# Other places in SBUF for the operands of TensorE, in a two-block fp32 kernel on one core

## The chip, the cores and the metric

The kernel runs on one NeuronCore of a Trainium2 chip. The metric is the device time of one execution in microseconds. Engines are named as in the profile: PE (TensorE, matrix products), PEld (the loads of TensorE's stationary operand), DVE (VectorE), ACT (ScalarE), POOL (GpSimd), SP (the queue that issues most transfers).

## What is computed

Two transformer-like blocks run one after the other on 256 tokens of width 2048, all in fp32. What takes the time is the products with large weight matrices. Cut to these:

```python
z   = rmsnorm(x) @ w_in                          # 2048 -> 3392, then convolution and attention
x   = x + rmsnorm(concat(conv, attn) @ w_out)
ff  = silu(h @ w_gate) * (h @ w_up) @ w_down     # width 5632
x   = x + rmsnorm(ff)
p   = rmsnorm(x) @ w_in_2                        # then a pooling mixer and a linear recurrence
h   = x + concat(y_pool, y_lru) @ w_out_2
q   = z @ peer_wq                                # keys of 16384 experts, 8 heads, top 16 of each
out = rmsnorm(h + sum_k gate * gelu(u[expert] . z) * v[expert])
```

The last line is computed densely: all 16384 rows of `peer_u` are multiplied with the tokens, a matrix of gates that is zero outside the chosen experts is multiplied in, and the result is multiplied with all rows of `peer_v`.

## The kernel before

**Three products for one.** TensorE takes the operands of the large products as fp32r. Each fp32 operand is split into two such parts, `hi` (a copy by ACT, L140) and `lo` (the rest, a subtraction by DVE, L143). A product of two fp32 matrices is then three: hi by hi, hi by lo, lo by hi. Weights stream from HBM through `raw` (three buffers), and `hi` and `lo` have four buffers of 1024 columns each.

**Two forms of product.** A matmul instruction holds one operand still (the stationary one, 128 columns, loaded by LDWEIGHTS: 512 B in each partition) and streams the other (the moving one). In `unit_a` (L165 to L167) the weights are stationary and the 256 tokens move, so a product has 256 columns, 1024 B in a partition:

```python
T.matmul(o, hi[:, c], xh[:, kt, :], ...)   # L165: stationary hi, moving xh
T.matmul(o, hi[:, c], xl[:, kt, :], ...)   # L166
T.matmul(o, lo[:, c], xh[:, kt, :], ...)   # L167
```

In `unit_b` (L179 to L181) and in `products` (L1122) it is the other way round: 128 tokens are stationary and 512 columns of weights move, 2048 B in a partition. In the profile's names `acc<-znh,hi` the moving tile stands first and the stationary one second.

**Stages, in order.** `w_in` and `w_out` (both forms, until about 365 us), `w_gu` (`unit_a`, moving `lhi`/`llo`, until 857 us), `w_down` (`unit_b`, stationary `acth`/`actl`, until 1115 us), `w_in_2` (both forms, `z2h`/`z2l`), `w_out_2` (`unit_b`, `lhi`/`llo`), `peer_wq` (`unit_a`, `lhi`/`llo`), `peer_u` (`unit_a`, moving `znh`/`znl`, 1464 to 2219 us), `peer_v` (`products`, stationary `wsp`, from 2219 us to the end). Beside them run small products in plain fp32, and during `peer_u`, from 1625 to 1999 us, 256 one-hot products `gps` (L1043: moving `hb`, stationary `ha`, 256 columns) that build the gates. They stand in pairs among the products of `peer_u`.

**What sets the order.** The code records background work (`bg`, `heads`) between pieces of the weight stream, and a scheduler then orders each engine's instructions by its own simulation of time. Each engine runs its list in that order. A tile's buffers (`bufs`) limit how far ahead a writer may run.

**What sets the places.** Pools are laid one behind the other in each partition, and tiles within a pool likewise, so a tile's byte address is the sum of all that was opened before it. `lslot` cuts a view of 4096 columns out of a slightly larger tile, from column `off`; `lhs(16)` gives the view that begins 16 columns (64 B) further on. All slices that TensorE takes step by whole multiples of 512 B, except in one small unit of 320 columns, so each operand has one residue of its address modulo 512.

Of the kernel before, what the change touches and what calls it, by code (L numbers as in the profile page):

```python
# [10 lines left out]
F32 = mybir.dt.float32  # L11
F32R = mybir.dt.float32r
# [33 lines left out]
def build(tc, t, out, dbg=None, stop=None):  # L46

    nc = tc.nc
    dbg = dbg or {}
    top = ExitStack()  # L50
# [3 lines left out]
    cpool = top.enter_context(tc.tile_pool(name="cpool", bufs=1))  # L54
    stream = top.enter_context(tc.tile_pool(name="stream", bufs=1))

    gap = top.enter_context(tc.tile_pool(name="gap", bufs=1)).tile([128, 16], F32, name="gap")
    nc.vector.memset(gap, 0.0)
    lpool = top.enter_context(tc.tile_pool(name="lpool", bufs=1))
    small = top.enter_context(tc.tile_pool(name="small", bufs=4))  # L60

    x1d = dram.tile([128, 2, D], F32, name="x1d")
    hd = dram.tile([128, 2, D], F32, name="hd")
# [15 lines left out]
    def pc(name, j, n=1):  # L79
        o = COLS[name][0]  # L80
        return par[:, o + j:o + j + n]
# [88 lines left out]
    def unit_b(ps, w, xh, xl, nkt, n=512, k0=0):  # L170


        acc = [ps.tile([128, 512], F32, tag="acc", name="acc", bufs=4) for _ in range(2)]
        for kt, hi, lo in w.kts(nkt, n):
            for c in range(2):
                o = acc[c][:, :n]
                s = slice(c * 128, c * 128 + 128)
                k = k0 + kt
                T.matmul(o, xh[:, k, s], hi, start=(kt == 0), stop=False)  # L179
                T.matmul(o, xh[:, k, s], lo, start=False, stop=False)  # L180
                T.matmul(o, xl[:, k, s], hi, start=False, stop=(kt == nkt - 1))  # L181
        return acc
# [56 lines left out]
    def split(hi, lo, src):  # L239
        A.activation(hi, src, AF.Copy)  # L240
        V.tensor_tensor(lo, src, hi.bitcast(F32), op=ALU.subtract)
# [35 lines left out]

    def lslot(tag, name, shape, dt=F32R, off=0):

        x = lpool.tile([128, 4128 if tag == "lhi" else 4112], dt, tag=tag, name=name)[:, off:off + 4096]  # L280
        k = dict(zip("abc", shape))
        return x.rearrange("p (a b c) -> p a b c", **k) if len(shape) == 3 else x.rearrange("p (a b) -> p a b", **k)

    def lhs(off=0):
        return lslot("lhi", "lhi", (16, 256), off=off), lslot("llo", "llo", (16, 256), off=off)


    ps = tc.tile_pool(name="ps1", bufs=1, space=PSUM)
# [20 lines left out]
    kvn = p0.tile([128, 4, 256], F32, name="kvn")  # L309

    xgh, xgl = lhs()
    xTs = [slot(n, [128, 8, 256], name=f"xT{n}") for n in ("attn", "vt")]
    xsq = slot("sq", [128, 2, 4, 256], name="xsq")
# [138 lines left out]
    for c in range(2):  # L452
        A.activation(junk[:, :512], kvraw[:, c, :], AF.Square, accum_out=ssk[:, c:c + 1])
    rk = rstd_col(ssk[:, :2], 512, 2)
    mixh, mixl = lhs(16)


# [217 lines left out]
    nc.gpsimd.dma_start(grow, t["post_mix_norm"].partition_broadcast(128))  # L675
    r = proj((unit_b(ps, w, mixh, mixl, 8, k0=8) for _ in range(4)), p2, y, grow, half)
    hh, hl = lhs()
    r = rows(p2, add_residual(y, r, xt, y), y, hh, hl, "pre_ffn_norm")
    _, rb2 = to_row(lpool, r, "rb")
    nc.gpsimd.dma_start(x1d, y)  # L680
    dump("x1", y)
    if stop == "x1":
# [8 lines left out]

    p3x = ExitStack()
    p3 = p3x.enter_context(tc.tile_pool(name="p3", bufs=1))
    acth, actl = (p3.tile([128, 11296], F32R, name=n)[:, 16:11280].rearrange("p (k t) -> p k t", k=44)
                  for n in ("acth", "actl"))
    p3t = p3x.enter_context(tc.tile_pool(name="p3t", bufs=2))
    opt["pool"] = 0
# [1 line left out]
    for u in range(22):  # L699
# [7 lines left out]
        split(acth[:, 2 * u:2 * u + 2, :], actl[:, 2 * u:2 * u + 2, :], sg)  # L707
    grow = p3.tile([128, D], F32, name="grow3")
    y = lslot("lhi", "y3", (2, D), F32)
    x1 = lslot("llo", "x1r", (2, D), F32)  # L710
    nc.gpsimd.dma_start(x1, x1d)
    nc.gpsimd.dma_start(grow, t["post_ffn_norm"].partition_broadcast(128))
# [14 lines left out]
    t4 = t4x.enter_context(tc.tile_pool(name="t4", bufs=2))  # L727
# [95 lines left out]
    for u in range(2):  # L823
        acc = unit_b(ps, w, zh, zl, 16)
        for c in range(2):
            A.activation(ut[:, c, 512 * u:512 * u + 512], acc[c], AF.Copy, scale=r2[:, c:c + 1])
        for g in (2 * u, 2 * u + 1):
            dT = t4.tile([128, 2, 256], F32, tag="dT", name="dT")
            for i in range(2):
                ch = slice(256 * g + 128 * i, 256 * g + 128 * i + 128)  # L830
                dp = ps.tile([128, 512], F32, tag="tr", name="dp", bufs=4)
                T.matmul(dp[:, :256], ut[:, 0, ch], band[:, g, 0:256], start=True, stop=False)
                T.matmul(dp[:, 128:256], ut[:, 1, ch], band[:, g, 256:384], start=False, stop=True)
                V.tensor_copy(dT[:, i, :], dp[:, :256])
            for jt in range(2):
                yp = ps.tile([128, 512], F32, tag="tr", name="yp", bufs=4)
                for i in range(2):
                    T.matmul(yp[:, :256], pw[:, g, i, 128 * jt:128 * jt + 128], dT[:, i, :],  # L838
                             start=(i == 0), stop=(i == 1))
                k = 2 * g + jt  # L840
                yt = t4.tile([128, 256], F32, tag="yt", name="yt")
                V.tensor_scalar(yt, yp[:, :256], pc("pool_b_2", k), pc("pool_scale_2", k),
                                op0=ALU.add, op1=ALU.mult)
                split(yh[:, k, :], yl[:, k, :], yt)
# [157 lines left out]
    G = {}  # L1002
# [10 lines left out]
    NT = 8  # L1013
    hot = {}

    def iota8():
        return iota[:, None, :].to_broadcast([128, NT, 128])

    def over(x, g):
        return x[:, NT * g:NT * g + NT, None].to_broadcast([128, NT, 128])  # L1020

    def hot_a(g):
        a = G["hot"].tile([128, NT, 128], F32R, tag="ha", name="ha")
        hot[g] = [a]
        V.tensor_tensor(a, iota8(), over(slotT[:, 0, :], g), op=ALU.is_equal)

    def hot_e(g):
        e = G["hot"].tile([128, NT, 128], F32, tag="he", name="he")
        hot[g].append(e)
        V.tensor_tensor(e, iota8(), over(slotT[:, 1, :], g), op=ALU.is_equal)  # L1030

# [27 lines left out]
    for g in range(S // NT + 1):  # L1059
        first, last = g == 0, g == S // NT  # L1060
        for i, fn in enumerate((lambda g=g: hot_a(g), lambda g=g: hot_e(g),
                                lambda g=g: hot_b(g, 0), lambda g=g: hot_b(g, 1))):
            if not last:
                bg.append((1250, fn))
            if not first:
                bg.append((0, lambda g=g, i=i: meet(g - 1, i)))
                if i:
                    bg.append((700, lambda g=g, i=i: store(g - 1, i - 1)))
        if not first:
            bg.append((700, lambda g=g: store(g - 1, 3)))  # L1070
# [53 lines left out]
    for b in range(32):  # L1124
# [6 lines left out]
        for i in range(4):  # L1131
            x = (wh[:, i, :], wl[:, i, :], b == 0 and i == 0, b == 31 and i == 3)
# [144 lines left out]
```

## Time and profile before

| | us |
|---|---|
| median of 3 runs | 2948.01 (2947.69 to 2949.89) |
| the profiled execution | 2947.42 |
| its span (first to last instruction) | 2945.6 |
| PE busy in the span | 2905.0 |
| DVE busy | 1899.1 |
| ACT busy | 1326.9 |

The profiled execution is 0.6 us from the median. PE is recorded as busy when at least one matmul is in flight; matmuls overlap, one of 256 columns being in flight for some 280 ns while the next begins some 115 ns after it. So the busy time says that PE has work, not how fast it goes. How fast it goes is the spacing: the time from the start of one matmul to the start of the next. It is read from the timeline, or from the count of matmuls in a long stretch.

### The profile page before, as it was taken

The page shows a single profiled execution, that of the slowest core. Times are in us where ns is not written, and L with a number is a line of the kernel's source. Part 1 is how long each engine was busy: PE and PEld are TensorE (multiplying, and loading weights), DVE is VectorE, ACT ScalarE, POOL GpSimd, SP SyncE. Part 2 cuts the span into 40 slices and gives each one's busy share as a digit, 9 for nine tenths or more (in the row PEclk, how much of TensorE's full clock was granted, in tenths as well). Part 3 has the DMA queues.
Part 4 walks back from the last instruction along what each step waited for, and adds up shares of the span by engine and source line. Part 5 has one row for each costly group of instructions (what it writes and reads, how often), then busy time and mean ns, then how long its engine had stood idle before and what let it go on. Part 6 is the DMA issues. An engine that isn't in the chain of part 4 may idle for free.

```text
span 2945.6 us, 45194 instructions
## 1 busy us (share of the span) xinstructions
PE 2905.0 (99%) x18950; PEld 2640.4 (90%) x18950; DVE 1899.1 (64%) x2532; ACT 1326.9 (45%) x1638; POOL 28.4 (1%) x45
## 2 busy tenths in 40 slices
PE   8999999999999999999999999999999999999998
PEld 8887799999998888888999999999998888888886
DVE  7976655555554447857997988885445555555554
ACT  6226544444443435545444444444444444444443
POOL 0000000000000000000000000000000000000000
PEclk9999999999999999999999999999999999999999
DMA  6443555555565555465555666668657676667663
GB/s 238 165 150 129 214 196 186 187 188 188 187 215 186 187 194 215 152 220 207 174 206 215 231 220 252 220 254 296 214 209 264 230 240 239 235 232 239 231 217 138
DMA packets 120253, 615.72 MB, mean 209 GB/s; under 512 B 10320, under 2 KB 43216, under 8 KB 54768
## 3 DMA queue, kind: packets, MB, share of 16 engines
q1 hardware_dynamic: 116656, 574.16, 55.8%
q0 software_dynamic: 3392, 38.67, 3.3%
q8 instruction: 148, 2.42, 0.3%
q14 instruction: 57, 0.47, 0.1%
HBM read 570.85 MB, written 41.94 MB: 208 GB/s over the span
## 4 chain that ended last, share of the span: by engine, by line
PE 71%; issue 25%; DVE 3%; ACT 1%; DMA 0%; POOL 0%; SPq 0%; DVEq 0%; POOLq 0%; ACTq 0%
PE acc L167 16%; PE acc L165 16%; PE acc L166 16%; PE acc L180 6%; PE acc L181 6%; PE acc L179 6%; PE acc L189 2%; PE gps L1043 1%; DVE lo L143 1%; PE acc L198 0%; ACT junk L656 0%; PE yp L838 0%; PE scp L922 0%; PE sp L515 0%; DMA raw<-w_in 0%
## 5 line engine op out<-in xcount | busy, mean ns | idle before, releaser
L143 DVE TENSOR_TENSOR lo<-raw,hi 128x1024 fp32r<-128x1024 f32 (+1 forms) x968 | 1177.1, 1219 | 904.5 <-ACT hi L140 902.7
L140 ACT ACTIVATE hi<-raw 128x1024 fp32r<-128x1024 f32 (+1 forms) x968 | 1021.6, 1057 | 1403.2 <-PE acc L166 716.0
L167 PE MATMUL acc<-znh,lo 128*128 128x256 f32 x2048 | 570.7, 281 | 1.9 <-DVE lo L143 1.7
L166 PE MATMUL acc<-znl,hi 128*128 128x256 f32 x2048 | 572.0, 280 | 0.0
L165 PE MATMUL acc<-znh,hi 128*128 128x256 f32 x2048 | 572.0, 280 | 0.0
L1122 PE MATMUL o<-hi,wsp 128*128 128x512 f32 x2048 | 559.3, 395 | 0.0
L165 PE MATMUL acc<-lhi,hi 128*128 128x256 f32 x1856 | 522.5, 282 | 10.5 <-ACT hi L140 9.5
L167 PE MATMUL acc<-lhi,lo 128*128 128x256 f32 x1856 | 522.5, 283 | 1.2 <-DVE lo L143 1.2
L166 PE MATMUL acc<-llo,hi 128*128 128x256 f32 x1856 | 518.7, 280 | 0.9 <-DVE llo L253 0.9
L1122 PEld LDWEIGHTS o<-hi,wsp 128*128 128x128 f32 x2048 | 385.8, 188 | 89.9
L165 PEld LDWEIGHTS acc<-znh,hi 128*128 128x128 f32 x2048 | 391.1, 191 | 0.0
L167 PEld LDWEIGHTS acc<-znh,lo 128*128 128x128 f32 x2048 | 382.8, 188 | 3.4 <-DVE lo L143 3.3
L166 PEld LDWEIGHTS acc<-znl,hi 128*128 128x128 f32 x2048 | 384.5, 188 | 0.0
L165 PEld LDWEIGHTS acc<-lhi,hi 128*128 128x128 f32 x1856 | 349.3, 188 | 11.3 <-ACT hi L140 9.7
L166 PEld LDWEIGHTS acc<-llo,hi 128*128 128x128 f32 x1856 | 351.6, 189 | 1.4 <-DVE llo L253 1.4
L167 PEld LDWEIGHTS acc<-lhi,lo 128*128 128x128 f32 x1856 | 348.4, 188 | 2.1 <-DVE lo L143 2.1
L1122 PE MATMUL o<-lo,wsp 128*128 128x512 f32 x1024 | 321.2, 395 | 0.0
L1122 PEld LDWEIGHTS o<-lo,wsp 128*128 128x128 f32 x1024 | 192.9, 188 | 45.0
L181 PE MATMUL acc<-hi,actl 128*128 128x512 f32 x352 | 139.7, 397 | 0.0
L180 PE MATMUL acc<-lo,acth 128*128 128x512 f32 x352 | 139.4, 396 | 0.0
L180 PE MATMUL acc<-lo,lhi 128*128 128x512 f32 (+1 forms) x352 | 137.2, 390 | 0.0
L179 PE MATMUL acc<-hi,acth 128*128 128x512 f32 x352 | 136.9, 389 | 0.0
(339 smaller groups left out, 2725.7 us busy)
## 6 DMA issues: line engine op xcount, KB each, us to landing
raw<-peer_u SPq DMA_DIRECT2D x128, 1024.0 KB, 5.0
raw<-peer_v SPq DMA_DIRECT2D x128, 1024.0 KB, 5.6
raw<-w_gu SPq DMA_DIRECT2D x88, 1024.0 KB, 4.9
raw<-w_in SPq DMA_DIRECT2D x47, 1024.0 KB, 4.9
raw<-w_down SPq DMA_DIRECT2D x44, 1024.0 KB, 4.9
raw<-w_out SPq DMA_DIRECT2D x32, 1024.0 KB, 4.9
raw<-peer_wq SPq DMA_DIRECT2D x16, 1024.0 KB, 4.8
hD<-hg SPq DMA_DIRECT2D x32, 512.0 KB, 3.2
```

The source lines that it names most:

```text
L140: A.activation(hi[:, :m], raw[:, o:o + m], AF.Copy)
L143: e.tensor_tensor(lo[:, :m], raw[:, o:o + m], hi[:, :m].bitcast(F32), op=ALU.subtract)
L165: T.matmul(o, hi[:, c], xh[:, kt, :], start=(kt == 0 and m % 2 == 0), stop=False)
L166: T.matmul(o, hi[:, c], xl[:, kt, :], start=False, stop=False)
L167: T.matmul(o, lo[:, c], xh[:, kt, :], start=False, stop=(kt == nkt - 1 and m % 2 == 1))
L179: T.matmul(o, xh[:, k, s], hi, start=(kt == 0), stop=False)
L180: T.matmul(o, xh[:, k, s], lo, start=False, stop=False)
L181: T.matmul(o, xl[:, k, s], hi, start=False, stop=(kt == nkt - 1))
L189: T.matmul(acc[m // 2][:, m % 2, :], v[:, m * 128:m * 128 + 128], x(kt), start=(kt == 0 and m % 2 == 0), stop=(kt == nkt - 1 and m % 2 == 1))
L1043: T.matmul(o[:, j, :, :], a[:, 2 * p + j, :], b[:, 2 * p + j, :, :], start=True, stop=True)
L1122: T.matmul(acc[c][o // 512 + q], x[:, s], v[:, 512 * q:512 * q + 512], start=st, stop=sp)
```

## The change

Nothing that is computed changes. Places of tiles in SBUF change, and two tiles have one buffer in place of two. The parts: a pool of 64 B (`gap`) is gone; the pool `small` is opened ahead of `lpool`; the tiles `lhi`, `acth`, `actl` and `ha` are a little longer, with the view begun 16 columns in where they are stationary; `llo` has no offset any more; `yt` (pool mixer) and `he` (one-hot work) have one buffer.

```diff
-    gap = top.enter_context(tc.tile_pool(name="gap", bufs=1)).tile([128, 16], F32, name="gap")
-    nc.vector.memset(gap, 0.0)
+    small = top.enter_context(tc.tile_pool(name="small", bufs=4))
     lpool = top.enter_context(tc.tile_pool(name="lpool", bufs=1))
-    small = top.enter_context(tc.tile_pool(name="small", bufs=4))
...
-        x = lpool.tile([128, 4128 if tag == "lhi" else 4112], dt, tag=tag, name=name)[:, off:off + 4096]
+        x = lpool.tile([128, 4224 if tag == "lhi" else 4096], dt, tag=tag, name=name)[:, off:off + 4096]
...
-        return lslot("lhi", "lhi", (16, 256), off=off), lslot("llo", "llo", (16, 256), off=off)
+        return lslot("lhi", "lhi", (16, 256), off=off), lslot("llo", "llo", (16, 256))
...
-    acth, actl = (p3.tile([128, 11296], F32R, name=n)[:, 16:11280].rearrange("p (k t) -> p k t", k=44)
+    acth, actl = (p3.tile([128, 11392], F32R, name=n)[:, 16:11280].rearrange("p (k t) -> p k t", k=44)
...
-                yt = t4.tile([128, 256], F32, tag="yt", name="yt")
+                yt = t4.tile([128, 256], F32, tag="yt", name="yt", bufs=1)
...
-        a = G["hot"].tile([128, NT, 128], F32R, tag="ha", name="ha")
+        a = G["hot"].tile([128, 1152], F32R, tag="ha", name="ha")[:, 16:1040].rearrange("p (t k) -> p t k", t=NT)
...
-        e = G["hot"].tile([128, NT, 128], F32, tag="he", name="he")
+        e = G["hot"].tile([128, NT, 128], F32, tag="he", name="he", bufs=1)
```

The residues modulo 512 of the operands' byte addresses, as the two programs place them (M moving, S stationary):

| products | operand | before | after | the other operand |
|---|---|---|---|---|
| `unit_a`, 256 columns | M `lhi` | 0 | 384 | S `hi`, `lo`: 448 in both |
| | M `llo`, `znh`, `znl`, `z2h`, `z2l` | 128 | 384 | S `hi`, `lo`: 448 |
| `gps`, 256 columns | M `hb` | 128 | 384 | S `ha`: 128 before, 448 after |
| `products` of `peer_v`, 512 columns | S `wsp` | 64 | 448 | M `hi`, `lo`: 448 |
| `unit_b` of `w_down` | S `acth` | 192 | 448 | M 448 |
| | S `actl` | 320 | 448 | M 448 |
| `unit_b` of `w_out`, `w_out_2` | S `lhi` | 64 | 448 | M 448 |
| | S `llo` | 192 | 384 | M 448 |
| `unit_b` of `w_in` | S `lhi` / `llo` | 0 / 128 | 384 / 384 | M 448 |
| `unit_b` of `w_in_2` | S `z2h`, `z2l` | 128 | 384 | M 448 |
| plain fp32, 256 columns | M `qn`, `kvn`, `x32` | 128 | 384 | S `raw`: 448 |

The change moves instructions at two places only, where the two tiles lose a buffer. On DVE in the pool mixer (`yt` is the mixer's output, `llo` its low part, `dT` and `xph` belong to the mixer and the recurrence beside it), before:

```order
L842 TENSOR_SCALAR yt<-yp,par 128x256 x2
L834 COPY dT<-dp 128x256 x2
L241 TENSOR_TENSOR llo<-yt,lhi 128x256 x2
L143 TENSOR_TENSOR lo<-raw,hi 128x1024
L842 TENSOR_SCALAR yt<-yp,par 128x256 x2
```

and after:

```order
L241 TENSOR_TENSOR llo<-yt,lhi 128x256
L834 COPY dT<-dp 128x256
L842 TENSOR_SCALAR yt<-yp,par 128x256
L834 COPY dT<-dp 128x256
L241 TENSOR_TENSOR llo<-yt,lhi 128x256
L842 TENSOR_SCALAR yt<-yp,par 128x256
L143 TENSOR_TENSOR lo<-raw,hi 128x1024
L241 TENSOR_TENSOR llo<-yt,lhi 128x256
```

Each `yt` is now followed by its own `llo` before the next `yt`; before, they went two by two. On DVE where the one-hot work begins (`ha`, `he` are comparisons with the slots, `hb` is `he` times the gates), before:

```order
L1025 TENSOR_TENSOR ha<-cst,slotT 128x1024
L1030 TENSOR_TENSOR he<-cst,slotT 128x1024
L1025 TENSOR_TENSOR ha<-cst,slotT 128x1024
L1030 TENSOR_TENSOR he<-cst,slotT 128x1024
L143 TENSOR_TENSOR lo<-raw,hi 128x1024
```

and after:

```order
L1025 TENSOR_TENSOR ha<-cst,slotT 128x1024
L1030 TENSOR_TENSOR he<-cst,slotT 128x1024
L1025 TENSOR_TENSOR ha<-cst,slotT 128x1024
L143 TENSOR_TENSOR lo<-raw,hi 128x1024
L241 TENSOR_TENSOR gatel<-slp,gateh 128x128 x2
```

The second `he` waits until the first has been used. Some of the `gps` pairs on PE stand a few rows earlier or later for it; their number is the same.

## Rows read from the trace of the kernel before

**Rows 1.** page, sections 1 and 2: busy us (share, instructions); clock in forty slices.

```profile
PE 2905.0 (99%) x18950; PEld 2640.4 (90%) x18950; DVE 1899.1 (64%) x2532; ACT 1326.9 (45%) x1638; POOL 28.4 (1%) x45
...
PEclk9999999999999999999999999999999999999999
```

**Rows 2.** waits of TensorE: who waited for what, us in total, times, longest.

```profile
PE tsp L249 <- issue: 10.2, 2, 5.4
...
PE acc L167 <- DVE lo L143: 2.9, 6, 0.7
```

**Rows 3.** windows: stretch, length, each engine's busy us (instructions), clock, DMA.

```profile
400.00:820.00 420.00, 420.00 (x3569) 420.00 (x3568) 227.63 (x221) 176.15 (x185) 0.00 (x0) 1.00 0.54 187
870.00:1070.00 200.00, 200.00 (x867) 163.72 (x866) 93.32 (x80) 80.65 (x85) 0.00 (x0) 1.00 0.57 197
1280.00:1330.00 50.00, 50.00 (x216) 40.22 (x215) 24.52 (x23) 21.21 (x27) 0.57 (x1) 1.00 0.62 225
1625.00:2219.00 594.00, 594.00 (x5041) 594.00 (x5040) 425.58 (x455) 276.81 (x379) 4.28 (x8) 1.00 0.66 236
2240.00:2900.00 660.00, 660.00 (x2841) 535.10 (x2841) 358.04 (x295) 279.02 (x268) 0.00 (x0) 1.00 0.67 232
```

**Rows 4.** groups by line: shape, count, busy us, mean ns of one, idle before.

```profile
L165 PE MATMUL acc<-lhi,hi 128*128 128x256 f32 x1856 | 522.5, 282 | 10.5 <-ACT hi L140 9.5 <-ACT lhi L252 0.9
...
L1122 PE MATMUL o<-hi,wsp 128*128 128x512 f32 x2048 | 559.3, 395 | 0.0
L1122 PE MATMUL o<-lo,wsp 128*128 128x512 f32 x1024 | 321.2, 395 | 0.0
...
L179 PE MATMUL acc<-hi,acth 128*128 128x512 f32 x352 | 136.9, 389 | 0.0
...
L179 PE MATMUL acc<-hi,lhi 128*128 128x512 f32 x320 | 124.2, 398 | 2.1 <-ACT lhi L491 2.1
...
L179 PE MATMUL acc<-hi,z2h 128*128 128x512 f32 x64 | 24.2, 398 | 0.0
```

**Rows 5.** timeline of TensorE around the first one-hot products: start, length.

```profile
1612.07 0.28 PE L167 MATMUL acc<-znh,lo 128*128 128x256 f32 x1
...
1624.65 0.28 PE L167 MATMUL acc<-znh,lo 128*128 128x256 f32 x1
1624.76 1.12 PE L1043 MATMUL gps<-hb,ha 128*128 128x256 f32 x8
1625.72 0.28 PE L165 MATMUL acc<-znh,hi 128*128 128x256 f32 x1
...
1626.43 0.28 PE L165 MATMUL acc<-znh,hi 128*128 128x256 f32 x1
```

**Rows 6.** timeline, 512-column products with z2h and z2l held.

```profile
1177.02 0.39 PE L179 MATMUL acc<-hi,z2h 128*128 128x512 f32 x1
...
1180.45 0.39 PE L179 MATMUL acc<-hi,z2h 128*128 128x512 f32 x1
```

**Rows 7.** timeline, 512-column products of w_down.

```profile
1000.06 0.40 PE L181 MATMUL acc<-hi,actl 128*128 128x512 f32 x1
1000.30 0.39 PE L179 MATMUL acc<-hi,acth 128*128 128x512 f32 x1
1000.52 0.40 PE L180 MATMUL acc<-lo,acth 128*128 128x512 f32 x1
1000.76 0.40 PE L181 MATMUL acc<-hi,actl 128*128 128x512 f32 x1
```

**Rows 8.** chain of waits: start, length, engine, line, count, plain fp32 products.

```profile
82.84 27.63 PE acc L189 x128
```

**Rows 9.** instructions of the tile yt: count, ns least/median/most, first and last.

```profile
L842 DVE TENSOR_SCALAR yt<-yp,par x8: 527/532/544, 1217.0 to 1237.9; 128x256 f32<-128x256 f32 x8
```

**Rows 10.** windows with the pool mixer and with the one-hot work.

```profile
1205.00:1262.00 57.00, 57.00 (x402) 53.36 (x401) 45.00 (x61) 28.72 (x39) 0.00 (x0) 1.00 0.44 151
1700.00:1800.00 100.00, 100.00 (x850) 100.00 (x849) 86.65 (x99) 48.70 (x73) 1.07 (x2) 1.00 0.64 237
```

## The prediction, made before the changed kernel ran

> **What bounds the kernel now.** I read the page first: PE has work in flight in 2905.0 us of a span of 2945.6, and the granted clock stands at nine tenths or more in all forty slices [rows 1]. Then the waits of PE: the longest group is 10.2 us, and what it loses to DVE's `lo` in the whole kernel is 2.9 us [rows 2]. So no other engine and no transfer holds the kernel; the rate at which matmuls follow each other does. That rate isn't in the busy time, since matmuls overlap (one of 256 columns is recorded as 282 ns long [rows 4]). It is in the spacing, and I took it from the counts in long stretches [rows 3], leaving out of each count the two (256 columns) or one (512) that were in flight when the stretch began:
>
> - `w_gu`, 256 columns: 420.0 us / 3567 = 117.7 ns
> - `peer_u` from 1625 us, 256 columns: 594.0 / 5039 = 117.9 ns
> - `w_down`, 512 columns: 200.0 / 866 = 230.9 ns
> - `w_out_2`, 512 columns: 50.0 / 215 = 232.6 ns
> - `peer_v`, 512 columns: 660.0 / 2840 = 232.4 ns
>
> Next I looked in the timeline for the same products at another rate, and this is the view on which the prediction rests [rows 5]. In `peer_u`, from 1612.07 to 1624.65 us, 111 products follow each other in 12.58 us: 113.3 ns. Then come eight `gps` products, which are recorded as one piece of 1.12 us: less the 0.28 us that the last one lasts, 0.84 / 7 = 120 ns. Behind them the same three products of `peer_u`, with the same tiles, shapes and buffers, take 0.71 / 6 = 118.3 ns, and the whole rest of the stage keeps to 117.9, although the last `gps` is at 1999 us. Nothing waits there: PE is busy in all of the 594.0 us. So there are two rhythms, the quick one is 4% quicker, and something in the `gps` products threw PE from one into the other.
>
> What sets them apart is the place: TensorE loads the next weights while a product streams (PEld is busy in 90% of the span [rows 1]), so two reads of SBUF run side by side. Take as distance the moving operand's residue less the stationary one's, modulo 512, from the table of the change. In `peer_u` it is 192 in all three products, and there the quick rhythm can stand. In `gps` it is 0, and the spacing is 120. In `w_gu` it goes 64, 192, 64, and the spacing is 117.7 throughout. Of the 512-column stages, `w_down` (256, 256, 128) shows steps of 0.24, 0.22 and 0.24 us [rows 7]; `w_in_2`, where it is 320 throughout, takes 3.43 us for 15 products, 228.7 ns [rows 6]; `peer_v`, 384 throughout, 232.4. Twice 113.3 is 226.7, and about that is the 0.22 of `w_down`; I take it for the least that a 512-column product can have here.
>
> **The change, part by part.** *256 columns.* All large stages and `gps` get one distance, 448 (64 B below). I forecast that a chain of products with one distance, and with no foreign distance in it, settles into the quick rhythm, as `peer_u` did until `gps` came. That distance itself isn't in the trace; the nearest rows are 120 (distance 0) above and 113.3 below, and I take the lower, since it is the row of an unmixed chain. `lhi`/`llo`: 3 x 1856 [rows 4] = 5568 products x (117.7 - 113.3 = 4.4 ns) = 24.5 us. `peer_u` from 1625 us, `gps` among them: 5039 x 4.6 = 23.2 us. The products that are quick already gain nothing. Together **-47.7 us**, all of it on the path, since PE is the path.
>
> *512 columns.* `wsp`, `acth` and `actl` get distance 0. No 512-column row has it. Bounds: 226.7 as above, and 226.7 + 6.7 = 233.4, if it costs them what it costs `gps` over the quick rhythm. I take 228.7, the unmixed chain of `w_in_2`. `peer_v`: (2048 + 1024) x (232.4 - 228.7 = 3.7) = 11.4 us. `w_down`: 3 x 352 x (230.9 - 228.7 = 2.2) = 2.3 us. Together **-13.7 us**. The 3 x 320 products of `w_in`, `w_out` and `w_out_2` keep a mixture or get a distance of 64; I leave them as they are (bounds: -5.9 x 960 = -5.7 us, and +0.8 x 960 = +0.8).
>
> *Plain fp32* products: 27.63 us / 128 = 215.9 ns [rows 8], far above the others per column. I leave them at that; a full step of 6.7 ns either way on some 340 of them is 2.3 us.
>
> *`yt` with one buffer.* DVE writes each `yt`, waits for ACT's copy, subtracts, and only then writes the next. Queued behind on DVE are the `lo` splits that L167 of PE waits for. At worst one `yt` (0.532 us, eight of them [rows 9]) is lost each time, 4.3 us; but DVE has 12.0 of 57.0 us free there and PE doesn't wait at all [rows 10], so four buffers of `lo` cover most of it. I take **+1 us**.
>
> *`he` with one buffer* costs nothing: writer and reader are both DVE, in order; only the first `gps` shift by a row or two. The missing memset of `gap` is nothing.
>
> *What is late next.* With PE 4% quicker, DVE's 86.65 of 100 us in the one-hot stretch [rows 10] become 90%. That is still under PE; the `lo` waits, 2.9 us now [rows 2], may double: **+2 us** (0 to 4). Transfers use 0.66 of the DMA engines [rows 3] and would use 0.69.
>
> Sum: -47.7 - 13.7 + 1 + 2 = -58.4 us, from the profiled 2947.4 to 2889.0; the median is 0.6 us above the profiled execution, so **2889.6 us**. With every product at its least and no give-back: -47.7 - 17.5 (`peer_v`, 5.7 x 3072) - 4.4 (`w_down`) - 5.7 = -75.3, so 2872.7.
>
> [...]
>
> **The rivals.** *Near is bad (slower).* Two read streams get into each other's way where their places are close. For it: the one row at distance 0 is the slowest of its kind (120), and in 512 columns the far distances 256 and 320 have the quickest rows; afterwards all are at 0 or 64 B, nearer than nearly everything before. Against it: in `w_gu` the sequence 64, 192, 64 holds 117.7, no worse than `peer_u` at 192 alone after `gps`; and which stream is ahead should matter, not only how far. Price at 120: `lhi`/`llo` 2.3 x 5568 = 12.8; `peer_u` 2.1 x 5039 = 10.6; the products that are quick today, 3 x 2048 + 256 - 5039 = 1361 at the start of `peer_u` and 3 x 256 with `z2h`/`z2l` by the program, 6.7 x 2129 = 14.3; 512 columns at 233.4: 1.0 x 3072 + 2.5 x 1056 = 5.7; in all +43, 2991 us. At 118.3, 1.3 over today's mean of 117.0 (5568 at 117.7, 5039 at 117.9, 2129 at 113.3), for 12,736 products: +17, and with the 5.7 +22, 2970 us. It decides from a mean 256-column spacing of 117.0 upwards.
>
> *Only one form gains.* The 256-column products settle and the 512-column ones pay 233.4: -47.7 + 5.7 + 3 = -39, 2909 us. Or the other way round: -13.7 + 1, 2935 us.
>
> *Places are worth nothing,* and the two rhythms come from the order in which products happen to start: 2948 us, within 5. The step at the first `gps` [rows 5] would then be that of any interruption. Against it: in `w_gu`, where the distances differ from product to product, 420 us pass at 117.7 with nothing between the products [rows 3].
>
> That the change doesn't do what it says is no rival, since the residues are those of the built program.
>
> **How the numbers follow.** A measurement of this kernel can tell about 0.2% from no change, 5.9 us. Forecast 0.45, own range 2873 to 2905 (least of all products; nothing at all from 512 columns); one form alone 0.20, 2909 to 2935; nothing 0.10; near is bad 0.25, 2960 to 2991. Faster is 0.45 + 0.20 = 0.65, same 0.10, slower 0.25. From 2868 to 2970 all but the upper half of the last case lies inside, some 0.85. The low end has 5 us for the plain fp32 products and the give-back.
>
> **What would show it.** Right: a spacing of 113.3 in `w_gu` and in `peer_u` through and behind the `gps`, and the `gps` themselves below 120; `peer_v` at or under 229. Wrong: 118 or more in `w_gu`; a `peer_u` that starts quick and is slow after `gps` (then the mixing wasn't the cause); `peer_v` at 233; waits of PE for `lo` of more than 6 us in all.

## The result, and the profile after

The changed kernel takes 2882.38 us (median of 4 runs, 2880.65 to 2882.98), the kernel before 2948.16 beside it: a ratio of 0.9775, interval 0.9758 to 0.9792. The forecast of 2889.6 was 7 us too high, and the forecast's own range, 2873 to 2905, holds the time. The profiled execution has a span of 2880.0 us against 2945.6, so 65.6 us less.

The page after (busy us, share, instructions; the clock in forty slices), as [rows 1] showed it of before:

```profile
PE 2840.0 (99%) x18950; PEld 2596.6 (90%) x18950; DVE 1896.9 (66%) x2531; ACT 1327.6 (46%) x1638; POOL 33.0 (1%) x45
...
PEclk9999999999999999999999999999999999999999
```

The same 18950 products at the same granted clock (0.995 of full speed over the span, 0.996 before) keep PE in flight for 65.0 us less. So nearly the whole gain is products that follow each other faster. The waits of TensorE after (who waited for what, us in total, times, longest) are nearly those of [rows 2]:

```profile
PE tsp L249 <- issue: 10.2, 2, 5.4
...
PE acc L167 <- DVE lo L143: 3.0, 6, 0.6
```

The stages, by windows of the trace after (stretch, length, each engine's busy us and instructions, clock, DMA); the first, second, sixth and last answer to [rows 3], the seventh to [rows 10]:

```profile
400.00:820.00 420.00, 420.00 (x3708) 420.00 (x3707) 234.97 (x231) 183.87 (x193) 0.00 (x0) 1.00 0.56 194
870.00:1070.00 200.00, 200.00 (x884) 165.68 (x883) 93.83 (x80) 82.29 (x86) 0.00 (x0) 1.00 0.56 195
1212.00:1249.00 37.00, 37.00 (x316) 37.00 (x315) 20.76 (x23) 17.89 (x20) 0.00 (x0) 1.00 0.53 180
1260.00:1330.00 70.00, 70.00 (x304) 56.91 (x303) 34.94 (x32) 30.21 (x37) 0.00 (x0) 1.00 0.61 220
1521.00:1583.00 62.00, 62.00 (x529) 62.00 (x528) 44.17 (x43) 27.83 (x29) 0.00 (x0) 1.00 0.64 229
1625.00:2160.00 535.00, 535.00 (x4723) 535.00 (x4723) 395.22 (x421) 258.98 (x351) 4.28 (x8) 1.00 0.68 247
1700.00:1800.00 100.00, 100.00 (x885) 100.00 (x884) 89.34 (x103) 50.35 (x78) 1.06 (x2) 1.00 0.70 252
2260.00:2860.00 600.00, 600.00 (x2649) 496.82 (x2648) 330.65 (x273) 258.29 (x247) 0.00 (x0) 1.00 0.67 231
```

Counted as before (two of 256 columns, or one of 512, in flight at the start are left out): `w_gu` 420.0 / 3706 = 113.3 ns (117.7 before), `peer_u` 535.0 / 4721 = 113.3 (117.9), `w_down` 200.0 / 883 = 226.5 (230.9), `peer_v` 600.0 / 2648 = 226.6 (232.4). Two stretches are still slow: 37.0 / 314 = 117.8 in the 256-column products of `w_in_2`, and 62.0 / 527 = 117.6 early in `peer_u`. And `w_out_2` stands at 70.0 / 303 = 231.0, near the 232.6 of [rows 3].

At the first one-hot products the step of [rows 5] is gone; timeline of TensorE after (start, length):

```profile
1596.03 0.28 PE L166 MATMUL acc<-znl,hi 128*128 128x256 f32 x1
1596.14 0.84 PE L1043 MATMUL gps<-hb,ha 128*128 128x256 f32 x6
1596.82 0.28 PE L167 MATMUL acc<-znh,lo 128*128 128x256 f32 x1
```

Six `gps` take 0.68 us from their start to the next product, 113.3 ns each, and `peer_u` goes on at that.

Where the 65.6 us come from can be read from the places at which each stage begins. Instructions of four tiles (count, ns least/median/most, first and last start), before:

```profile
L179 PE MATMUL acc<-hi,acth x352: 389/389/393, 865.8 to 1109.2; 128*128 128x512 f32 x176
L165 PE MATMUL acc<-z2h,hi x256: 276/276/562, 1118.4 to 1273.2; 128*128 128x256 f32 x128
L165 PE MATMUL acc<-znh,hi x2048: 276/281/369, 1464.4 to 2219.0; 128*128 128x256 f32 x187
L1122 PE MATMUL o<-hi,wsp x2048: 388/393/404, 2219.4 to 2933.0; 128*128 128x512 f32 x187
```

and after:

```profile
L179 PE MATMUL acc<-hi,acth x352: 389/389/392, 845.4 to 1084.1; 128*128 128x512 f32 x176
L165 PE MATMUL acc<-z2h,hi x256: 276/281/562, 1093.3 to 1249.5; 128*128 128x256 f32 x128
L165 PE MATMUL acc<-znh,hi x2048: 276/276/367, 1436.8 to 2171.0; 128*128 128x256 f32 x187
L1122 PE MATMUL o<-hi,wsp x2048: 388/389/395, 2171.3 to 2867.4; 128*128 128x512 f32 x187
```

| stretch | before, us | after, us | gain |
|---|---|---|---|
| start to `w_down` (`w_in`, `w_out`, `w_gu`) | 865.8 | 845.4 | 20.4 |
| `w_down`, to `w_in_2` | 252.6 | 247.9 | 4.7 |
| `w_in_2`, `w_out_2`, `peer_wq` | 346.0 | 343.5 | 2.5 |
| `peer_u` | 755.0 | 734.5 | 20.5 |
| `peer_v` to its last product | 713.6 | 696.1 | 17.5 |

Together that is 65.6 us, all of it; behind the last product both kernels have 12.6 us.

### The profile page after: what moved, and what is told of

Read it like the earlier page. It is cut to its first block, busy times and chain, and to the rows that moved or that the text cites. A ratio compares the mean times of both kernels' runs of the same rounds, so it can differ in the third digit from the quotient of the medians.

```text
span 2880.0 us, 45191 instructions
## 1 busy us (share of the span) xinstructions
PE 2840.0 (99%) x18950; PEld 2596.6 (90%) x18950; DVE 1896.9 (66%) x2531; ACT 1327.6 (46%) x1638; POOL 33.0 (1%) x45
## 4 chain that ended last, share of the span: by engine, by line
PE 71%; issue 25%; DVE 3%; ACT 1%; DMA 0%; POOL 0%; SPq 0%; DVEq 0%; POOLq 0%
PE acc L167 16%; PE acc L166 16%; PE acc L165 16%; PE acc L180 6%; PE acc L179 6%; PE acc L181 6%; PE acc L189 3%; PE gps L1043 1%; DVE lo L143 1%; PE acc L198 0%; PE scp L922 0%; PE yp L838 0%; DMA raw<-w_in 0%; PE sp L515 0%; PE tsp L249 0%
## 5 line engine op out<-in xcount | busy, mean ns | idle before, releaser
L167 PE MATMUL acc<-znh,lo 128*128 128x256 f32 x2048 | 564.7, 277 | 2.0 <-DVE lo L143 1.8
L165 PE MATMUL acc<-znh,hi 128*128 128x256 f32 x2048 | 565.5, 277 | 0.0
L166 PE MATMUL acc<-znl,hi 128*128 128x256 f32 x2048 | 565.5, 277 | 0.0
L1122 PE MATMUL o<-hi,wsp 128*128 128x512 f32 x2048 | 547.7, 389 | 0.0
L165 PE MATMUL acc<-lhi,hi 128*128 128x256 f32 x1856 | 514.6, 278 | 9.5 <-ACT hi L140 9.1
L167 PE MATMUL acc<-lhi,lo 128*128 128x256 f32 x1856 | 512.9, 277 | 1.3 <-DVE lo L143 1.2
L165 PEld LDWEIGHTS acc<-znh,hi 128*128 128x128 f32 x2048 | 385.2, 188 | 0.0
L1122 PE MATMUL o<-lo,wsp 128*128 128x512 f32 x1024 | 315.4, 389 | 0.0
```

The lines of the kernel that those rows point to most:

```text
L165: T.matmul(o, hi[:, c], xh[:, kt, :], start=(kt == 0 and m % 2 == 0), stop=False)
L166: T.matmul(o, hi[:, c], xl[:, kt, :], start=False, stop=False)
L167: T.matmul(o, lo[:, c], xh[:, kt, :], start=False, stop=(kt == nkt - 1 and m % 2 == 1))
L1122: T.matmul(acc[c][o // 512 + q], x[:, s], v[:, 512 * q:512 * q + 512], start=st, stop=sp)
```

## The experiments

The theory is that of the prediction: a chain of products with one distance, whichever, goes quick, and a foreign distance inside it throws it out. *Distance* is the moving operand's residue less the stationary one's. The rivals that the result leaves standing: the distance itself is what counts; the absolute place counts; the new order (`yt`, `he` with one buffer) did it. Each run is one kernel; where there is only one execution of a kernel, the stages are compared by their spacing, which the long windows give to 0.1 ns.

### The distance itself

`gap` is put back with 16, 32, 48, 64 or 96 columns, which shifts all moving operands of 256-column products and the held `lhi`, `wsp`, `acth` together; `ha` is cut so that `gps` has the same distance as `peer_u`. Every long chain keeps one distance throughout, as in the changed kernel. The edit for the smallest:

```diff
+    gap = top.enter_context(tc.tile_pool(name="gap", bufs=1)).tile([128, 16], F32, name="gap")
+    nc.vector.memset(gap, 0.0)
     small = ...
-        a = ...tile([128, 1152], ...)[:, 16:1040]...
+        a = ...tile([128, 1152], ...)[:, 0:1024]...
```

Distance 0 for 256 columns, 448 for 512 columns (16 columns of `gap`):

> The changed kernel with all tiles behind the weights' stream 64 B further on, so that every 256-column product has distance 0 (moving less stationary residue, modulo 512) and the 512-column ones with wsp, acth and actl have 448; gps go with the others. Theory A (one distance throughout a chain is what counts, which distance matters little): 113.3 ns in w_gu and peer_u, 226.7 in w_down and peer_v, 2882 us within 8. Theory B (the particular distance counts; 0 is the one at which gps took 120 ns before): 120 ns in w_gu and peer_u, 6.7 x 12,700 = +85 us, and the 512-column products between 226.7 and 233.4, 0 to +28: 2960 to 2995 us. Theory C (only the distance modulo 128 counts): slow in both forms, like B.

It took 2983.14 us, 31.6 more than the kernel before on the same chip (2951.57). Its windows:

```profile
400.00:820.00 420.00, 420.00 (x3502) 420.00 (x3502) 224.85 (x218) 173.08 (x182) 0.00 (x0) 1.00 0.53 183
...
1625.00:2160.00 535.00, 535.00 (x4461) 535.00 (x4460) 404.41 (x441) 248.50 (x350) 4.28 (x8) 1.00 0.64 233
2260.00:2860.00 600.00, 600.00 (x2573) 483.73 (x2572) 324.84 (x268) 253.00 (x242) 0.00 (x0) 1.00 0.68 237
```

420.0 / 3500 and 535.0 / 4459 are 120.0 ns in `w_gu` and `peer_u`, and 600.0 / 2572 is 233.3 in `peer_v`. One distance, unmixed, and slower than these stages were before: the first half of the theory (any one distance goes quick) falls. The `gps` of before at 120 [rows 5] had shown the price of distance 0.

Distance 192 for 256 columns, 256 for 512 columns (64 columns of `gap`, `ha` from column 80):

> The same with 256 B: every 256-column product at distance 192, the distance of peer_u in the kernel before, but now with gps at 192 too; 512-column ones with wsp, acth and actl at 256. Theory A: quick throughout, peer_u stays at 113.3 through the gps since these are no foreign distance any more; 2882 us within 8. Theory B: 117.9 ns in w_gu and peer_u (4.6 x 12,700 = 58 us), 512 columns at some 231: 2940 to 2965 us. Theory C: distances differ from the changed kernel's by 256, a multiple of 128, so no change: 2882 us.

It took 2882.05 us, as the changed kernel. Its windows have the counts of the changed kernel, one for one:

```profile
400.00:820.00 420.00, 420.00 (x3708) 420.00 (x3708) 234.82 (x231) 184.12 (x193) 0.00 (x0) 1.00 0.57 194
...
1625.00:2160.00 535.00, 535.00 (x4723) 535.00 (x4722) 395.34 (x421) 258.95 (x351) 4.27 (x8) 1.00 0.67 247
2260.00:2860.00 600.00, 600.00 (x2649) 496.82 (x2648) 331.01 (x273) 258.54 (x247) 0.00 (x0) 1.00 0.67 231
```

Distances 448 and 192 (113.3 ns), and 0 and 256 (226.6 ns), give the same spacings: they agree modulo 256, though not modulo 512. Then the other values:

Distance 64 / 384 (32 columns, `ha` from column 112):

> Tiles behind the weights' stream 128 B further on than in the changed kernel: every 256-column product at distance 64, the 512-column ones with wsp, acth and actl at 384. So far 0 was slow (120 and, in 512 columns at 448, 233.3 ns) and 192 was as quick as 448. Theory A, narrowed to modulo 128 (one distance throughout, 64 modulo 128 in 256 columns and 0 modulo 128 in 512): 113.3 and 226.7, 2882 us, or some 20 more if a long stage happens to start in the slow rhythm. Theory E (modulo 256; 64 isn't 192): 117.7 in w_gu and peer_u as lhi had at 64 before, +55 us; 232.4 in peer_v, which had 384 throughout before, and in w_down, +24 us; 2955 to 2965 us.

Distance 128 / 320 (48 columns, `ha` from column 96):

> 192 B further on: 256-column products at distance 128, 512-column ones at 320. Modulo 128 this is the case of distance 0: 120 and 233.3 ns, 2983 us within 5. Modulo 256 it is a new one: 256 columns anywhere from 113.3 to 120, and 512 columns near the 228.7 that w_in_2 had at 320 in the kernel before (+8 us): 2890 to 2975 us.

Distance 320 / 128 (96 columns, `ha` from column 48):

> 384 B further on: 256-column products at distance 320, 512-column ones at 128. If distances count modulo 256 (or 128), the spacings of all long stages are those of the kernel at 64 and 384, within 0.2 ns, and the time within 5 us of it. If they count modulo 512, they differ; 320 lies between 192 and 448, which are both quick, so 113.3 would be likely, 2882 to 2910 us.

They took 2937.76, 2954.41 and 2939.33 us; before, on that chip, 2949.66. Neither forecast for 64 / 384 holds as a whole: `w_gu` has the quick spacing, `peer_u` and `peer_v` the slow one. Windows of the first (64 / 384):

```profile
400.00:820.00 420.00, 420.00 (x3708) 420.00 (x3707) 235.61 (x231) 183.24 (x192) 0.00 (x0) 1.00 0.57 194
...
1625.00:2160.00 535.00, 535.00 (x4545) 535.00 (x4544) 392.28 (x423) 251.63 (x347) 4.27 (x8) 1.00 0.65 238
2260.00:2860.00 600.00, 600.00 (x2573) 482.97 (x2572) 323.91 (x267) 253.24 (x242) 0.00 (x0) 1.00 0.68 233
```

of the second (128 / 320):

```profile
400.00:820.00 420.00, 420.00 (x3541) 420.00 (x3541) 226.42 (x220) 175.19 (x184) 0.00 (x0) 1.00 0.54 184
...
1625.00:2160.00 535.00, 535.00 (x4511) 535.00 (x4510) 405.82 (x441) 250.97 (x351) 4.27 (x8) 1.00 0.65 235
2260.00:2860.00 600.00, 600.00 (x2623) 492.87 (x2622) 333.29 (x275) 257.62 (x246) 0.00 (x0) 1.00 0.69 238
```

and of the third (320 / 128), in these stages the like of the first within one product:

```profile
1625.00:2160.00 535.00, 535.00 (x4544) 535.00 (x4544) 394.09 (x424) 251.45 (x346) 4.28 (x8) 1.00 0.65 238
2260.00:2860.00 600.00, 600.00 (x2573) 482.94 (x2572) 323.82 (x268) 252.70 (x242) 0.00 (x0) 1.00 0.68 233
```

So 64 and 320 are one distance too. What the long windows of these kernels show, modulo 256:

| distance modulo 256 | 256 columns, ns | 512 columns, ns |
|---|---|---|
| 0 | 120.0 | 226.6 |
| 64 | 113.3 in `w_gu`, 117.8 in `peer_u` | 228.8 |
| 128 | 118.7 | 233.3; 232.4 in the kernel before |
| 192 | 113.3, or 117.8 in some stretches | 233.3 |

A short stretch of `peer_u` in the trace at 128 / 320 has another mean: 67 products from 1542.88 to 1550.92 us, behind a wait, 120.0 ns each; the 511 products ahead of it, from 1481.90 us, are at 118.7. That doesn't show a second spacing. A stretch of 67 products between two waits in `peer_u` of the changed kernel, from 1504.41 to 1512.49 us, has a mean of 120.6 although nearly all its steps are 0.11 or 0.12 us: the step behind the wait takes 0.20 there, and two products recorded as one piece take 0.59 to the next.

The kernel before fits in, but for one row: its `w_in_2` at 320 (64) took 228.7 [rows 6], the step inside `w_down` with 256 (0) on both sides 0.22 us [rows 7], and its `gps` at 0 took 120 [rows 5]. Its `peer_v` at 384 took 232.4 [rows 3], though, and the kernel at 64 / 384, with the same residues modulo 512, takes 233.3. So the distance doesn't fix the 512-column spacing to the last nanosecond either; what makes this difference is open.

### The foreign distance

The changed kernel with `gps` alone put at distance 0 (`ha` from column 0, as in the diff above, no `gap`):

> The changed kernel with one part undone: the stationary ha of the gps begins at the start of its tile, so the 256 gps have distance 0 again and all else keeps 448 and 0. Theory A (a foreign distance throws the chain out of the quick rhythm for good): peer_u 117.9 ns from the first gps to its end, 4.6 x 5000 = +23 us, 2905 us. Theory B (at 448 the chain is quick by itself): the gps take 120 ns, 1.7 us in all, and peer_u is back at 113.3 behind each pair: 2884 us.

It took 2905.84 us, 23.8 more than the kernel with distance 192 / 256 on the same chip, whose stages are those of the changed one. Timeline of TensorE at its first `gps`:

```profile
1596.93 0.28 PE L166 MATMUL acc<-znl,hi 128*128 128x256 f32 x1
1597.05 0.88 PE L1043 MATMUL gps<-hb,ha 128*128 128x256 f32 x6
1597.76 0.28 PE L167 MATMUL acc<-znh,lo 128*128 128x256 f32 x1
```

Six `gps` now take 0.71 us, 118.3 each, and from there on `peer_u` runs at 535.0 / 4539 = 117.9, by the window behind it:

```profile
1625.00:2160.00 535.00, 535.00 (x4541) 535.00 (x4539) 386.19 (x414) 250.98 (x344) 4.27 (x8) 1.00 0.65 238
```

4.5 ns on the 5070 or so products from 1597 to 2195 us is 23 us, the whole difference. Then the same thing the other way round: the kernel before with only `ha` moved, so that `gps` has the 192 of `peer_u` (`he` with one buffer makes the room):

```diff
-        a = G["hot"].tile([128, NT, 128], F32R, tag="ha", name="ha")
+        a = G["hot"].tile([128, 1152], F32R, tag="ha", name="ha")[:, 80:1104].rearrange("p (t k) -> p t k", t=NT)
...
-        e = G["hot"].tile([128, NT, 128], F32, tag="he", name="he")
+        e = G["hot"].tile([128, NT, 128], F32, tag="he", name="he", bufs=1)
```

> The kernel before with one part of the change alone: the stationary ha of the 256 gps at residue 448, so that their distance is 192 as that of the peer_u products around them (and one buffer for he, to make room). Everything else keeps its old place. Theory A (the foreign distance of the gps threw peer_u out of the quick rhythm): peer_u stays at 113.3 through the gps to its end, -22 us, 2926 us; all other stages as before. Theory F alone (any break draws the rhythm anew, whatever its distance): peer_u is slow after the first gps as before or after one of the 128 pairs, 2940 to 2949 us.

It took 2926.09 us, 23.6 less than before (median 2949.67, 2946.43 to 2951.89). Two of its windows:

```profile
400.00:820.00 420.00, 420.00 (x3568) 420.00 (x3568) 227.22 (x221) 176.15 (x185) 0.00 (x0) 1.00 0.55 186
...
1625.00:2160.00 535.00, 535.00 (x4723) 535.00 (x4722) 410.07 (x442) 261.81 (x361) 4.27 (x8) 1.00 0.68 247
```

`w_gu` as before, `peer_u` at 113.3 to its end. For `peer_u` this half of the theory is shown from both sides: `gps` at the chain's own distance leave it quick (113.3 ns), `gps` at 0 leave it slow (117.9). No other foreign distance was tried there.

### The order

The kernel before with one buffer for `yt` and `he`, and every operand of TensorE at its old place:

> The kernel before with only the two tiles yt and he at one buffer, every place of TensorE's operands as it was. If the changed order on DVE costs or brings nothing, as the comparison of the two traces says: 2948 us within 2. My forecast had +1 for yt and nothing for he. If the order had a part in the gain: 2940 or less.

It took 2951.62 us, within the range of before, and `peer_u` has 4541 products in the window from 1625 to 2160 us, where before has 4540. The order brings nothing that can be seen.

### The absolute place, and what a break does

All operands moved by 192 B together, distances as in the changed kernel (48 columns of `gap` opened ahead of the weights' pool):

> The changed kernel with the weights' stream and everything behind it 192 B further on: all distances as in the changed kernel, all residues themselves 192 higher. If only distances count, as A, B and C all say: 2882 us within 4, spacings as in the changed kernel. Theory D (the place itself counts, 384 for the moving and 448 for the stationary operand): another time, up to some 2950 us.

It took 2904.58 us, 22.5 more than the kernel with distance 192 / 256 beside it. `w_gu` is slow at 420.0 / 3566 = 117.8, `peer_u` quick, and `peer_v` has the 2649 products of the changed kernel in the window from 2260 to 2860 us:

```profile
400.00:820.00 420.00, 420.00 (x3568) 420.00 (x3568) 228.20 (x222) 175.62 (x184) 0.00 (x0) 1.00 0.54 187
...
1625.00:2160.00 535.00, 535.00 (x4723) 535.00 (x4723) 407.27 (x439) 261.08 (x359) 4.27 (x8) 1.00 0.68 246
```

I had not expected that. Either the place counts after all, or a chain at this distance has two rhythms and keeps the one in which it begins. The two slow stretches of the changed kernel speak for the second. The one in `peer_u` begins behind a wait, by the timeline of the changed kernel (in brackets the idle time before an instruction and who ended it):

```profile
1518.81 0.28 PE L166 MATMUL acc<-znl,hi 128*128 128x256 f32 x1
1519.48 0.39 PE L167 MATMUL acc<-znh,lo 128*128 128x256 f32 x1 [0.39 <-DVE lo L143]
...
1584.13 0.71 PE L989 MATMUL slp<-cst,sel 128*128 128x128 f32 x5
```

Before 1518.81 the steps are 0.11 us; behind the wait 62 us pass at 117.6, and behind the five plain fp32 products `slp` at 1584.13 it is 113.3 again. To tell the two apart, one plain fp32 product of 128 columns (recorded as two matmuls) is put ahead of five of the units of `w_gu` in that slow kernel, its result unused, no place changed:

```diff
+        if u in (4, 8, 12, 16, 20):
+            T.matmul(ps.tile([128, 512], F32, tag="tr", name="kick", bufs=4)[:, :128], ones, ident, start=True, stop=True)
```

> The kernel with everything 192 B further on (all distances as in the changed kernel), in which w_gu ran its whole 503 us in the slow rhythm, 117.8 ns, while peer_u was quick. Added: one plain fp32 product of 128 columns on PE ahead of units 4, 8, 12, 16 and 20 of w_gu's 22, whose result is not used (some 0.3 us each, 1.5 us in all). Theory F (at these distances both rhythms can hold; a break in the chain draws one anew, and it lasts until the next break): at one or more of the five breaks w_gu goes over to 113.3 and stays there at least until the next one; the time falls by up to 15 us below 2904.6. Theory D (the place itself makes w_gu slow): back to 117.8 within some ten products behind each break, 2906 us.

It took 2897.62 us. The added products start at 456.9, 544.2, 634.9, 722.2 and 812.9 us; the windows between them:

```profile
400.00:456.00 56.00, 56.00 (x478) 56.00 (x477) 29.03 (x29) 23.27 (x24) 0.00 (x0) 1.00 0.55 186
462.00:543.00 81.00, 81.00 (x717) 81.00 (x717) 44.04 (x44) 34.99 (x36) 0.00 (x0) 1.00 0.56 191
548.00:634.00 86.00, 86.00 (x733) 86.00 (x732) 45.65 (x44) 35.87 (x38) 0.00 (x0) 1.00 0.55 187
640.00:721.00 81.00, 81.00 (x717) 81.00 (x716) 44.03 (x44) 34.98 (x36) 0.00 (x0) 1.00 0.57 191
728.00:812.00 84.00, 84.00 (x715) 84.00 (x715) 44.13 (x43) 34.91 (x36) 0.00 (x0) 1.00 0.54 183
818.00:840.00 22.00, 22.00 (x197) 22.00 (x196) 12.46 (x14) 9.54 (x10) 0.00 (x0) 1.00 0.58 193
```

117.6, 113.3, 117.6, 113.3, 117.8 and, in a short stretch, 112.8 ns: each of the five turned the rhythm over. With the same tiles at the same places both rhythms occur, so the absolute place doesn't fix them; a break can turn one into the other, and between two breaks the rhythm stayed as it was.

Not every break does. In the changed kernel three groups of 8, 8 and 16 plain fp32 matmuls stand in a quick chain at 1417.97, 1419.33 and 1442.11 us, and it is quick ahead of the first (113.3 ns from 1397.79 to 1417.85 us) and behind the second (113.4 from 1420.34 to 1441.99 us) and the third (113.4 from 1444.01 to 1485.16 us). Nor does the same break always have the same outcome. In a second execution of the changed kernel (2879.56 us, with the same wait for `lo` at 1519.64 us) the stretch that was slow in the first is quick:

```profile
1521.00:1583.00 62.00, 62.00 (x549) 62.00 (x548) 45.63 (x46) 28.87 (x31) 0.00 (x0) 1.00 0.65 231
```

That is 62.0 / 547 = 113.3 ns where the first execution (2881.80 us) had 117.6. The 20 products more are worth 2.3 us, and the two executions differ by 2.2.

This puts the gain of `w_gu` in doubt too: did its mixture of 64 and 192 hold it slow in the kernel before, or had it only begun in the slow rhythm, as here? No run separates the two, but the timelines speak for the mixture. With the places of before (three traces: before and the two kernels above that change only `ha` or the buffers), `lhi`/`llo` move at 64, 192, 64 in `w_in`, `w_out`, `w_gu` and `peer_wq`; of 45 stretches of 20 or more products between breaks all 45 are slow. At 192 or 448 throughout, 65 of 78 such stretches in the same part of the program are quick in five traces (the changed kernel twice, and those with 192 / 256, with `gps` at 0 and, below, with `llo` moved), though only 4 of 16 in the kernel shifted by 192 B. And in the kernel before the chain passes from `lhi`/`llo` to `znh`/`znl`, from the mixture to 192, without a wait:

```profile
1464.30 0.28 PE L167 MATMUL acc<-lhi,lo 128*128 128x256 f32 x1
1464.42 0.28 PE L165 MATMUL acc<-znh,hi 128*128 128x256 f32 x1
...
1469.66 0.28 PE L166 MATMUL acc<-znl,hi 128*128 128x256 f32 x1
```

The 144 products from 1447.47 to 1464.42 us follow each other at 117.7 ns; some six products later it is 113.3, for the 40 from 1465.12 to 1469.66.

### A further step, and the changed kernel again

In `w_out` and `w_out_2` of the changed kernel `llo` still stands 64 B from the weights. Given `lhi`'s offset, it has distance 0 as well:

```diff
-        x = lpool.tile([128, 4224 if tag == "lhi" else 4096], ...
+        x = lpool.tile([128, 4224], ...
...
-        return lslot("lhi", ..., off=off), lslot("llo", "llo", (16, 256))
+        return lslot("lhi", ..., off=off), lslot("llo", "llo", (16, 256), off=off)
```

> The changed kernel with llo, too, begun 64 B further in where it is stationary (w_out, w_out_2), so that these 512-column products have distance 0 throughout in place of 0, 0 and 64. One distance, and that one quick: 226.7 in w_out_2 in place of 231.1 (384 products, 1.7 us) and the same in w_out (384 products, 1.6 us): 3 us below the changed kernel, ratio to the kernel before some 0.9765, if the stages behind keep their rhythms; if a later long stage starts in the slow one, up to 20 us more.

> The changed kernel once more, for the comparison with the version that moves llo: ratio to the kernel before 0.9775, 2882 us.

The first took 2878.47 us (2876.42 to 2879.83; ratio to before 0.9757, interval 0.9743 to 0.9771), the changed kernel beside it 2881.77 (2877.79 to 2882.58; 0.9767, interval 0.9753 to 0.9781). The window of the first:

```profile
1260.00:1330.00 70.00, 70.00 (x310) 58.01 (x309) 34.79 (x33) 31.25 (x38) 0.00 (x0) 1.00 0.61 220
```

70.0 / 309 = 226.5 against 231.0. On all 3 x 320 products of these two stages and of `w_in` 4.5 ns would be 4.3 us, and `w_in` keeps its distance here, so less; the medians differ by 3.3, but the intervals overlap. The spacing shows the gain, the time alone doesn't.

## Why the prediction was right, and where it was not

**The bound.** Right: only the spacing changed, and no wait took the place of what was won.

**256 columns.** Forecast 24.5 and 23.2 us. 113.3 was reached in `w_gu` and through the `gps`. By stretches: the products of `w_in`, `w_out` and `w_gu` (3 x 1600 of the 3 x 1856, the other 3 x 256 being `peer_wq`'s) should have given 21.1 and gave 20.4; `peer_u` gave 20.5. What is missing there is the slow stretch from 1521 to 1583 us (4.3 x 527 = 2.3 us), where the kernel before, between its waits, was quick. `z2h`/`z2l` went slow for 37 us (4.5 x 314 = 1.4 us), and that is part of why the third stretch gave 2.5 and not the 3.4 of `peer_wq` alone.

**512 columns: the term that was mis-sized.** Forecast 11.4 and 2.3; measured 17.5 and 4.7, which are the forecast's lower bounds (17.5 and 4.4). I took 228.7, "the unmixed chain of `w_in_2`", for products that measured 226.5 and 226.6. The runs show that 228.7 is the price of a distance of 64 modulo 256, and that 0 costs 226.6. The row for 0 was in the trace of before: the 0.22 of `w_down` [rows 7], at 256 on both sides. I missed it because I reckoned modulo 512, as the change does, and so thought that no 512-column row had the new distance.

**What was to be given back.** +1 for `yt` and +2 for `lo`: neither can be seen. The waits for `lo` are 3.0 us against 2.9, though DVE went to 89.3 of 100 us in the one-hot stretch, as reckoned (90%); the kernel before with one buffer for `yt` and `he` stays within the range of before.

**The step of the reasoning that failed.** "A chain of products with one distance, and with no foreign distance in it, settles into the quick rhythm": that a foreign distance of 0 throws `peer_u` out is shown from both sides; that any one distance goes quick is wrong. At 0 and 128 an unmixed chain of 256 columns has 120.0 and 118.7, at 64 or 192 it can have 113.3, and at both it can also be slow (117.8) for hundreds of microseconds. I said that the distance itself isn't in the trace and took the lower row "since it is the row of an unmixed chain". The reason was false; the value was right by luck, because 448 and 192, the distance of that row, are the same modulo 256. With the theory as put, the kernel at distance 0 should have been as quick; it was 31.6 us slower than before. And the forecast knew nothing of a second rhythm at the new distance: the same distances with all operands 192 B further on took 2904.58 us, at the very end of its range, because `w_gu` stayed slow.

**The rivals.** *Near is bad* named the right price for 256 columns at distance 0: 120 was forecast from `gps`, 120.0 was measured, and the kernel at 0 took 2983.14 where this rival, of the changed kernel, had said up to 2991. But 64 B below doesn't act as near (113.3), and for 512 columns the nearest place is the best (226.6 at 0, against 228.8 to 233.3). *Places are worth nothing* falls: with only places changed, the same products of `w_gu` and `peer_u` go from 113.3 ns in the changed kernel to 120.0 in the one at distance 0. What inside the chip does it isn't shown. What this rival said of interruptions was half right: a break can change the rhythm, at the same places. But in the chains at 192 and 448 it took `gps` at 0 to leave all of the rest of `peer_u` slow (117.9 ns).

**The difference of runs.** The same program gave 2877.79 to 2882.58 us. For the two executions with a trace the difference, 2.2 us, is that one stretch of `peer_u` which begins behind a wait in one rhythm or the other; for the rest it is likely, but not shown.

## What to carry to other kernels

Where one engine is busy all the time, read its rate from the count in long windows, stage by stage, and look in the trace for the same instruction at another rate: the few nanoseconds between (here 113.3 against 117.9 ns in `peer_u`) are a gain to look for, and the place where it jumps names a suspect. Where a value for a new setting is missing, ask by which period the machine could repeat before calling a row foreign; two rows of this trace gave the right value once taken modulo 256 (113.3 ns at 192 for 448, 0.22 us at 256 for 0). And give a small chain of products that stands inside a long one the same distance as its surroundings: where the 256 products `gps` stand, some 30 us of work in all, decided over 23 us of `peer_u` (23.8 and 23.6 us in the two runs).

## What was not expected of the hardware

- In the runs of this kernel the spacing of two products goes with the moving residue less the stationary one, modulo 256 B: 113.3, 117.8, 118.7 or 120.0 ns for 256 columns and 226.6, 228.8 or 233.3 for 512, and the best distance isn't the same for the two (64 or 192 against 0). That it counts modulo 256 is read from the pairs of distances that were run: 192 and 448, 64 and 320, 0 and 256 agree within one product in their long windows. It is in the single instruction too: `gps` is recorded as 276 ns long in the changed kernel and as 283 at distance 0, its weight load as 188 and 192.
- At one and the same distance, 192, a chain of 256 columns has two rhythms, 113.3 and 117.8. It keeps the one that it has, for over 400 us without a break (113.3 in the window of 420 us in `w_gu` of the changed kernel, 117.8 in the same window of the kernel shifted by 192 B), and one plain fp32 product turned it over five times out of five (117.6, 113.3, 117.6, 113.3, 117.8, 112.8); other breaks left it as it was (113.3 and 113.4 on the two sides), and the wait at 1519 us turned it in one execution of the same program (117.6) and not in the other (113.3). At distance 64 both spacings were seen too: 113.3 in `w_gu`, 117.8 in `peer_u`.
- Left open: what inside the chip makes the two rhythms, why a wait or a product of another kind turns them over on one occasion and not on another, why `peer_v` at 384 took 232.4 ns in one kernel and 233.3 in another, and whether a chain at 0 or 128 has a second rhythm that wasn't met. Nor was it tried whether an added product where the two slow stretches of the changed kernel begin (about 1212 and 1519 us) would win back the 3.7 us lost there.
